# Products of 64 rows in the two halves of TensorE's array, one transposition for two heads, and a second buffer for reloaded tiles

## The chip, the cores and the metric

One core of a Trainium2 chip runs the kernel once. The metric is the device time of that execution in microseconds; the time before is the median of three runs. Times inside a run come from one profiled execution. Engines are named as in the profile: PE is TensorE (PEld its weight loads), DVE is VectorE, ACT is ScalarE, POOL is GpSimd, SP is SyncE, whose queue issues most DMA transfers. Each engine works through its own list of instructions in a fixed order and waits where data or a buffer is not there yet.

## What is computed

One layer of an encoder: normalization and one wide projection, then three groups of heads side by side (attention to a memory, a convolution module, and two-way RWKV-7 time mixing), an output projection with residual, a mixture of 16 experts of which each takes 128 of the 1024 tokens, and a last normalization. The change touches the time mixing alone, and the residual that runs beside it. Per head the reference is a scan over time:

```python
def step(state, inp):
    r_t, w_t, k_t, v_t, kk_t, a_t = inp
    sa = jnp.einsum('bhij,bhj->bhi', state, -kk_t)
    state = (state * w_t[..., None, :]
             + sa[..., :, None] * (kk_t * a_t)[..., None, :]
             + v_t[..., :, None] * k_t[..., None, :])
    y_t = jnp.einsum('bhij,bhj->bhi', state, r_t)
    return state, y_t
```

It runs forward and backward over 1024 tokens for 6 heads of 64, and both results are added.

## The kernel before

**Chunks and units.** The scan is cut into chunks of C = 64 tokens. Two heads share the 128 partitions: head 0 of a pair in the lower 64 (`lo`), head 1 in the upper 64 (`hi`). A unit is one pair of heads and one half of the sequence for each direction d, with HC = 8 chunks per direction; 3 pairs and 2 halves make 6 units, u = 0 to 5. For each unit these steps run:

- `prep` makes AR (the columns that read the state, for both heads) and BK (b and k, the columns that write it, decayed to the chunk's start). BK before holds [partition, chunk, head, i, 64], and in head h's place only h's 64 partitions are filled; the other 64 were cleared once with POOL memsets (lines 668 and 669) and stay zero.
- `within` (line 845) makes the products within a chunk. A group is four chunks of one direction (q, d), four groups to a unit. For each head it takes a PSUM tile psA out of two buffers, fills it with four products of all 128 partitions (line 854; the zero half of BK picks the head), and DVE multiplies it by the mask of causality into AM (line 857).
- `prep2` transposes BK chunk by chunk and head by head on PE (line 870), ACT copies the result to BT (line 871), and v is brought into the layout of SV.
- `invert` inverts the triangular part of AM: ACT gathers blocks (line 895), DVE runs 31 steps of two instructions (lines 910 and 911), PE joins the blocks (lines 934 and 945).
- `chain` carries the state through 8 chunks, in three steps of PE each (psX, psSA, psS) with copies and additions on DVE and ACT in between (Xs, SV, S).

**The residual.** `residual` (line 1067) multiplies the first five blocks of the mixed heads, kept in DRAM as oT_d in a high and a low part, by the output projection: 4 column quarters of 8 token tiles, 32 tiles. Each tile loads two fo tiles (line 1083: fo0 from oT_d's high part, fo1 from the low), and the input part fx (line 1085); PE forms 15 products (lines 329 to 331), DVE adds fx (line 1089), and SP stores the sum (line 1090). FOB is the number of buffers of each fo tile.

**The order.** All steps are generators. A small planner, `run`, goes through the main steps (projections, then the chains of units 0 to 5, 24 steps each) and advances each filling step (within, invert, prep, prep2, residual) by its share of a window of main steps given by the R_ constants. The framework then sets each engine's final order from what was recorded. While chain u runs, PE's list thus mixes it with the products of unit u + 1, the preparation of u + 2 and the residual's tiles.

Of the kernel before, what the change touches and what calls it, by code (L numbers as in the profile page):

```python
# [12 lines left out]
F32 = mybir.dt.float32  # L13
# [3 lines left out]
ALU = mybir.AluOpType  # L17
# [3 lines left out]
P = 128  # L21
# [10 lines left out]
C = 64  # L32
NCH = S // C
HC = NCH // 2
# [12 lines left out]
    _n += _w  # L47
NPC = _n

FOB = 1  # L50
RW = 1
LB = 1
KB = 2
# [1 line left out]
FL = [0, 0, 0, 0, 0, 0, 0, 0]  # L55
# [45 lines left out]
def hybrid_block_kernel(ctx: ExitStack, tc: tile.TileContext, x, xT, memT, memn, w_in, w_mk, w_mv, pcols,  # L101
                        ups, gate_up, w_out, g_ffn, g_fin, w_router, w_eg, w_eu, w_ed, out, dbg=None):
    nc = tc.nc
    V, A, G, T = nc.vector, nc.scalar, nc.gpsimd, nc.tensor
# [12 lines left out]
    ident = const.tile([P, P], F32, name="ident")  # L117
# [16 lines left out]
    mask = const.tile([P, 2, C], F32, name="mask")  # L134
# [86 lines left out]
    def mm(tagp="mm", w=512, shape=None, name="mm", bufs=None):  # L221
        return psums[-1].tile(shape or [P, w], F32, name=name, tag=tagp, bufs=bufs or mmb[0].get(tagp))
# [270 lines left out]
    for n in range(2):  # L493
        ps = mm()
# [157 lines left out]
    Z = {}  # L652

    def early():

        ph1r.close()
        Z["se"] = pool("se", bufs=2, stack=ph2r, side="right")
        Z["pcs"] = [Z["se"].tile([P, 2, HC], F32, name=f"pcs{i}", bufs=1) for i in range(3)]
        Z["s1"] = pool("s1", bufs=2, stack=ph2e, side="right")
        Z["ew"] = pool("ew", bufs=1, stack=ph2e, side="right")  # L660
        ge = pool("ge", stack=ph2e, side="right")
        Z["AR"] = [ge.tile([P, 2, HC, 2, C], F32, name="AR0")]
        Z["AM"] = [ge.tile([P, 4, 2, 2, C], F32, name=f"AM{i}") for i in range(4)]
        Z["TT"] = [ge.tile([P, NCH, 2, 32], F32, name="TT0")]

        Z["BK"] = [ge.tile([P, HC, 2, 2, C], F32, name=f"BK{d}") for d in range(2)]
        for bk in Z["BK"]:
            G.memset(bk[hi, :, 0], 0.0)
            G.memset(bk[lo, :, 1], 0.0)
        Z["ep"] = ge.tile([P, HC, C + 1], F32, name="ep")  # L670
        G.memset(Z["ep"][:, :, 0:1], 1.0)
        Z["dinit"] = dinit = ge.tile([P, 16, 32], F32, name="dinit")
        G.iota(dinit, pattern=[[-2, 16], [1, 32]], base=0, channel_multiplier=0,
               allow_small_or_imprecise_dtypes=True)
        V.tensor_scalar(dinit, dinit, lpar1, None, op0=ALU.is_equal)

        rst = ge.tile([P, HC, C], F32, name="rst")
        V.memset(rst, 1.0)
        V.memset(rst[:, :, 0:1], 0.0)
        Z["rst"] = rst.rearrange("p a b -> p (a b)")  # L680
        yield
# [93 lines left out]
    def prep(p, k, g):  # L775
# [7 lines left out]
        for d in range(2):  # L783
# [36 lines left out]
            yield  # L820

            BK = g["BK", d] = Z["BK"][d]
            V.tensor_mul(BK[lo, :, 0, 0, :], kd[lo], cl[lo])
            (G, V)[FL[7]].tensor_mul(BK[hi, :, 1, 1, :], kd[hi], cl[hi])
            for r_, h, i in ((lo, 0, 1), (hi, 1, 0)):
                V.scalar_tensor_tensor(BK[r_, :, h, i, :], sg[r_], -0.5, cl[r_], op0=ALU.mult, op1=ALU.mult)  # L826
            yield
            both = chunks(pd["prod"][:, half(n)], d)
            if k == 0:
# [15 lines left out]
    def within(g):  # L845

        for q, d in ((0, 0), (0, 1), (1, 0), (1, 1)):
            AM = g["AM", d, q] = Z["AM"][g["u"] % 2 * 4 + q * 2 + d]
            for h in range(2):
                ps = mm("A", shape=[P, 4, 2, C], name="psA", bufs=2)  # L850
                r_ = slice(h * 64, h * 64 + 64)
                for c in range(4):
                    cc = q * 4 + c
                    T.matmul(ps[:, c].rearrange("p a b -> p (a b)"),  # L854
                             lhsT=g["BK", d][:, cc, h].rearrange("p a b -> p (a b)"),
                             rhs=g["AR"][:, d, cc].rearrange("p a b -> p (a b)"), start=True, stop=True)
                V.tensor_tensor(AM[:, :, h], ps, mask[:, None].to_broadcast([P, 4, 2, C]), op=ALU.mult)
                yield

    def prep2(p, k, g):  # L860
        BT = g["BT"] = Z["BT"][g["u"] % 2]
        SV = g["SV"] = Z["SV"][g["u"] % 2]
        for d in range(2):
            n = k if d == 0 else 1 - k

            for h in range(2):
                ps = mm(shape=[P, HC, C])
                r_ = slice(h * 64, h * 64 + 64)
                for cc in range(HC):
                    T.transpose(ps[:, cc, :], g["BK", d][r_, cc, h].rearrange("p a b -> p (a b)"), ident[r_, r_])  # L870
                A.copy(BT[:, d, :, h, :], ps)
                yield

            vt = load(f"v{p}", n, 1)
            if d == 1:
                vr = Z["sp"].tile([P, 512], F32, name="vr", bufs=1)
                G.tensor_scalar(vr, vt[:, ::-1], 1.0, None, op0=ALU.mult)
                vt = vr
            ps = mm(shape=[P, HC, C])
            for c in range(HC):  # L880
                for r_ in (lo, hi):
                    T.matmul(ps[r_, c, :], lhsT=vt[r_, c * C:(c + 1) * C], rhs=ident[r_, r_], start=True, stop=True)
            A.copy(SV[lo, d, :, 0, :], ps[lo])
            A.copy(SV[hi, d, :, 1, :], ps[hi])
            yield
# [762 lines left out]
```

## Time and profile before

| what | value |
|---|---|
| median of 3 runs | 1496.11 us (1487.31 to 1499.1) |
| profiled execution | 1507.9 us, span 1506.2 us |
| PE busy | 1350.8 us, 90% of the span |
| PE weight loads busy | 1063.8 us, 71% |
| DVE busy | 1180.6 us, 78% |
| ACT busy | 809.0 us, 54% |
| POOL busy | 266.2 us, 18% |

The profiled execution has its own time, a little above the median; a sum made from its rows is to be held against 1507.9 us. PE's clock is granted at one of two levels, 1.2 or 2.4 GHz, and the profile gives the share of full speed in each stretch: about 1.0 in the expert stage and 0.76 to 0.89 in most of the RWKV stage. A float32 product stands as two records on PE, a transposition as one, and a record's duration contains its way through the array, so records that overlap are counted by their starts and ends.

The program has three stages: the projections up to about 360 us, with convolution, attention and the first unit's preparation; the six units up to about 850 us; routing and experts until the end.

### The profile page before, as it was taken

What the parts mean: (1) busy time and instruction counts of PE and PEld (TensorE: products, weight loads), DVE (VectorE), ACT (ScalarE), POOL (GpSimd) and SP (SyncE); (2) the same over time, 40 slices, a digit from 0 to 9 for tenths busy, and PEclk for the clock granted to TensorE, in tenths of its full rate; (3) what the DMA queues carried; (4) which work ended last, traced back from release to release, by engine and by line L of the source; (5) the groups of instructions that cost most, each with busy time, mean ns of one, the idle gap of its engine ahead of it and who ended that gap; (6) DMA issues with size and microseconds to landing.
All of it is one profiled execution on the core that took longest, in us unless ns stands there. A gap on an engine that the chain in (4) does not pass through costs nothing.

```text
span 1506.2 us, 24148 instructions
## 1 busy us (share of the span) xinstructions
PE 1350.8 (90%) x9178; PEld 1063.8 (71%) x9178; DVE 1180.6 (78%) x2089; ACT 809.0 (54%) x1200; POOL 266.2 (18%) x238
## 2 busy tenths in 40 slices
PE   6888999997899888878999729999999999999995
PEld 4776657675777776667868628877777778877772
DVE  7899975699687869596833679988888888878875
ACT  4222574433535243433322418888787887767774
POOL 2233223432121212130221000000001101111000
PEclk9999999998889788887999859999999999999998
DMA  8222112412443433342473758999999999999975
GB/s 290 71 62 65 64 64 105 140 70 72 140 142 107 140 104 120 89 120 86 137 268 141 293 181 322 374 356 379 380 380 368 378 379 381 371 355 356 378 281 201
DMA packets 146100, 327.91 MB, mean 218 GB/s; under 512 B 9792, under 2 KB 64960, under 8 KB 145984
## 3 DMA queue, kind: packets, MB, share of 16 engines
q1 hardware_dynamic: 139360, 303.14, 54.9%
q0 software_dynamic: 6192, 22.55, 5.2%
q8 instruction: 72, 1.18, 0.3%
q10 hardware_dynamic: 432, 0.68, 0.1%
q14 instruction: 44, 0.36, 0.1%
HBM read 288.58 MB, written 37.75 MB: 217 GB/s over the span
## 4 chain that ended last, share of the span: by engine, by line
PE 62%; DVE 21%; ACT 5%; DMA 5%; issue 4%; POOL 1%; SPq 0%; POOLq 0%; ACTq 0%; DVEq 0%
PE mm L330 14%; PE mm L329 14%; PE mm L331 14%; PE mm L1455 3%; DVE cv L517 3%; DVE dtmp L910 2%; DVE Dt L911 2%; PE mm L1438 2%; DMA fo<-oT_d 2%; PE psA L854 1%; ACT Ld L895 1%; PE mm L745 1%; PE mm L1165 1%; PE psS L988 1%; DVE BK L826 1%
## 5 line engine op out<-in xcount | busy, mean ns | idle before, releaser
L1355 DVE SCALAR_TENSOR_TENSOR ewl<-eraw,pc,ewh 128x1024 fp32r<-128x1024 f32 x256 | 319.7, 1280 | 72.8 <-ACT ewh L1354 65.8
L1354 ACT ACTIVATE ewh<-eraw,pc 128x1024 fp32r<-128x1024 f32 x256 | 288.6, 1150 | 47.6 <-PE mm L331 46.2
L330 PE MATMUL mm<-ewl,xh 128*128 128x512 f32 x512 | 202.0, 394 | 1.7 <-DVE ewl L1355 1.6
L329 PE MATMUL mm<-ewh,xh 128*128 128x512 f32 x512 | 200.3, 409 | 1.0 <-ACT ewh L1354 1.0
L331 PE MATMUL mm<-ewh,xl 128*128 128x512 f32 x512 | 200.1, 391 | 0.0
L329 PE MATMUL mm<-hh,wh 128*128 128x512 f32 x304 | 127.0, 418 | 10.2 <-ACT hh L310 10.2
L330 PE MATMUL mm<-hl,wh 128*128 128x512 f32 x304 | 126.9, 417 | 0.2
L331 PE MATMUL mm<-hh,wl 128*128 128x512 f32 x304 | 126.2, 415 | 0.8 <-POOL wl L325 0.8
L330 PEld LDWEIGHTS mm<-ewl,xh 128*128 128x128 f32 x512 | 96.6, 189 | 26.1 <-DVE ewl L1355 5.2
L329 PEld LDWEIGHTS mm<-ewh,xh 128*128 128x128 f32 x512 | 96.3, 188 | 24.3 <-issue 4.1
L1351 DVE TENSOR_TENSOR ewl<-eraw,ewh 128x1024 fp32r<-128x1024 f32 x90 | 106.1, 1220 | 7.0 <-ACT ewh L1350 5.5
L331 PEld LDWEIGHTS mm<-ewh,xl 128*128 128x128 f32 x512 | 96.3, 188 | 20.0 <-DVE xl L1443 0.2
L1350 ACT ACTIVATE ewh<-eraw 128x1024 fp32r<-128x1024 f32 x90 | 92.5, 1058 | 10.8 <-PE mm L331 9.3
L1483 POOL DMA_INDIRECT x_d<-ye,idx x15 | 25.8, 1722 | 345.8 <-ACT ye L1482 345.8
L325 POOL TENSOR_TENSOR wl<-wraw,wh 128x512 fp32r<-128x512 f32 x38 | 57.9, 1527 | 129.2 <-ACT wh L324 111.4
L329 PEld LDWEIGHTS mm<-hh,wh 128*128 128x128 f32 x304 | 59.7, 196 | 26.5 <-ACT hh L310 10.7
L330 PEld LDWEIGHTS mm<-hl,wh 128*128 128x128 f32 x304 | 59.8, 197 | 18.0 <-DVE hl L311 2.9
L910 DVE TENSOR_TENSOR dtmp<-Lt,Dt 128x126 f32<-128x126 f32 (+22 forms) x186 | 70.5, 379 | 2.7
L517 DVE SCALAR_TENSOR_TENSOR cv<-u,cw,cv 128x512 f32<-128x512 f32 (+1 forms) x87 | 72.2, 860 | 0.1
L331 PEld LDWEIGHTS mm<-hh,wl 128*128 128x128 f32 x304 | 59.8, 197 | 16.3 <-POOL wl L325 3.2
L330 PE MATMUL mm<-ewl,fh 128*128 128x512 f32 x180 | 70.8, 393 | 0.1
L331 PE MATMUL mm<-ewh,fl 128*128 128x512 f32 x180 | 70.1, 389 | 0.0
(421 smaller groups left out, 2969.4 us busy)
## 6 DMA issues: line engine op xcount, KB each, us to landing
eraw<-in_w_eg_dram SPq DMA_DIRECT2D x64, 1024.0 KB, 10.2
eraw<-in_w_eu_dram SPq DMA_DIRECT2D x64, 1024.0 KB, 10.7
eraw<-in_w_ed_dram SPq DMA_DIRECT2D x64, 1024.0 KB, 8.1
fo<-oT_d SPq DMA_DIRECT2D x64, 320.0 KB, 3.9
wraw<-in_w_in_dram SPq DMA_DIRECT2D x38, 256.0 KB, 2.8
ld_k<-d_k SPq DMA_DIRECT2D x18, 256.0 KB, 3.3
ld_v<-d_v SPq DMA_DIRECT2D x18, 256.0 KB, 3.4
xk<-in_xT_dram SPq DMA_DIRECT2D x16, 256.0 KB, 4.9
```

Of the source, the lines that this page charges most:

```text
L325: G.tensor_sub(wl, raw, wh.bitcast(F32))
L329: T.matmul(ps, lhsT=lh, rhs=rh, start=first, stop=False)
L330: T.matmul(ps, lhsT=lh, rhs=rl, start=False, stop=False)
L331: T.matmul(ps, lhsT=ll, rhs=rh, start=False, stop=last)
L517: V.scalar_tensor_tensor(o[:, 0:ln], z, w, o[:, 0:ln], op0=ALU.mult, op1=ALU.add)
L910: IE.tensor_tensor(tmp[:, sg, ts], lcol, drow, op=ALU.mult)
L911: IE.tensor_tensor(Dt[:, sg, ts], Dt[:, sg, ts], tmp[:, sg, ts], op=ALU.add)
L1350: A.activation(h, raw[a], AF.Copy)
L1351: V.tensor_sub(l, raw[a], h.bitcast(F32))
L1354: A.activation(h, raw[a], AF.Copy, scale=gain)
L1355: V.scalar_tensor_tensor(l, raw[a], gain, h.bitcast(F32), op0=ALU.mult, op1=ALU.subtract)
L1455: T.matmul(acc[n], lhsT=xw[:, k - KT + NWHOLE], rhs=h[:, sl], start=k == 0, stop=k == KT - 1)
```

## The change

BK loses its head dimension: head 0's b and k stand in the lower 64 partitions of [partition, chunk, i, 64], head 1's in the upper 64, nothing is zero, and the memsets go. In `within`, both heads' PSUM tiles are taken at once, and the eight products of a group run over 64 partitions each, alternating between the lower and the upper half; the two masks follow. In `prep2`, one transposition of 128 by 128 turns both heads of a chunk, four chunks to a PSUM tile, and two copies per direction remain. The freed memory holds a second buffer for each fo tile (FOB = 2).

```diff
--- before.py
+++ after.py
@@ -47,7 +47,7 @@
     _n += _w
 NPC = _n
 
-FOB = 1
+FOB = 2
 RW = 1
 LB = 1
 KB = 2
@@ -662,11 +662,7 @@
         Z["AR"] = [ge.tile([P, 2, HC, 2, C], F32, name="AR0")]
         Z["AM"] = [ge.tile([P, 4, 2, 2, C], F32, name=f"AM{i}") for i in range(4)]
         Z["TT"] = [ge.tile([P, NCH, 2, 32], F32, name="TT0")]
-
-        Z["BK"] = [ge.tile([P, HC, 2, 2, C], F32, name=f"BK{d}") for d in range(2)]
-        for bk in Z["BK"]:
-            G.memset(bk[hi, :, 0], 0.0)
-            G.memset(bk[lo, :, 1], 0.0)
+        Z["BK"] = [ge.tile([P, HC, 2, C], F32, name=f"BK{d}") for d in range(2)]
         Z["ep"] = ge.tile([P, HC, C + 1], F32, name="ep")
         G.memset(Z["ep"][:, :, 0:1], 1.0)
         Z["dinit"] = dinit = ge.tile([P, 16, 32], F32, name="dinit")
@@ -820,10 +816,10 @@
             yield
 
             BK = g["BK", d] = Z["BK"][d]
-            V.tensor_mul(BK[lo, :, 0, 0, :], kd[lo], cl[lo])
-            (G, V)[FL[7]].tensor_mul(BK[hi, :, 1, 1, :], kd[hi], cl[hi])
-            for r_, h, i in ((lo, 0, 1), (hi, 1, 0)):
-                V.scalar_tensor_tensor(BK[r_, :, h, i, :], sg[r_], -0.5, cl[r_], op0=ALU.mult, op1=ALU.mult)
+            V.tensor_mul(BK[lo, :, 0, :], kd[lo], cl[lo])
+            (G, V)[FL[7]].tensor_mul(BK[hi, :, 1, :], kd[hi], cl[hi])
+            for r_, i in ((lo, 1), (hi, 0)):
+                V.scalar_tensor_tensor(BK[r_, :, i, :], sg[r_], -0.5, cl[r_], op0=ALU.mult, op1=ALU.mult)
             yield
             both = chunks(pd["prod"][:, half(n)], d)
             if k == 0:
@@ -846,15 +842,15 @@
 
         for q, d in ((0, 0), (0, 1), (1, 0), (1, 1)):
             AM = g["AM", d, q] = Z["AM"][g["u"] % 2 * 4 + q * 2 + d]
+
+            ps = [mm("A", shape=[P, 4, 2, C], name="psA", bufs=2) for h in range(2)]
+            for c in range(4):
+                for h, r_ in ((0, lo), (1, hi)):
+                    T.matmul(ps[h][:, c].rearrange("p a b -> p (a b)"),
+                             lhsT=g["BK", d][r_, q * 4 + c].rearrange("p a b -> p (a b)"),
+                             rhs=g["AR"][r_, d, q * 4 + c].rearrange("p a b -> p (a b)"), start=True, stop=True)
             for h in range(2):
-                ps = mm("A", shape=[P, 4, 2, C], name="psA", bufs=2)
-                r_ = slice(h * 64, h * 64 + 64)
-                for c in range(4):
-                    cc = q * 4 + c
-                    T.matmul(ps[:, c].rearrange("p a b -> p (a b)"),
-                             lhsT=g["BK", d][:, cc, h].rearrange("p a b -> p (a b)"),
-                             rhs=g["AR"][:, d, cc].rearrange("p a b -> p (a b)"), start=True, stop=True)
-                V.tensor_tensor(AM[:, :, h], ps, mask[:, None].to_broadcast([P, 4, 2, C]), op=ALU.mult)
+                V.tensor_tensor(AM[:, :, h], ps[h], mask[:, None].to_broadcast([P, 4, 2, C]), op=ALU.mult)
                 yield
 
     def prep2(p, k, g):
@@ -863,12 +859,11 @@
         for d in range(2):
             n = k if d == 0 else 1 - k
 
-            for h in range(2):
-                ps = mm(shape=[P, HC, C])
-                r_ = slice(h * 64, h * 64 + 64)
-                for cc in range(HC):
-                    T.transpose(ps[:, cc, :], g["BK", d][r_, cc, h].rearrange("p a b -> p (a b)"), ident[r_, r_])
-                A.copy(BT[:, d, :, h, :], ps)
+            for q in range(2):
+                ps = mm(shape=[P, 4, P])
+                for c in range(4):
+                    T.transpose(ps[:, c, :], g["BK", d][:, q * 4 + c].rearrange("p a b -> p (a b)"), ident)
+                A.copy(BT[:, d, q * 4:q * 4 + 4].rearrange("p c h t -> p c (h t)"), ps)
                 yield
 
             vt = load(f"v{p}", n, 1)
```

The order of instructions moves as follows. First SP, in the residual, tiles 4 and 5 (fo_3732 and fo_3849 are the high parts of tiles 4 and 5, each with its low part under the next number; the stores are those of tiles 3 and 4). Before:

```order
L1083 DMA fo_3732<-oT_d_134 128x5x128
L1090 DMA xacc_d<-fx 128x256
L1083 DMA fo_3733<-oT_d_135 128x5x128
L729 DMA ld_k_3559<-d_k_146 128x512
L729 DMA ld_r_3561<-d_r_147 128x512
L1085 DMA fx<-in_x_dram 128x256
L729 DMA ld_v_3877<-d_v_145 128x512
L1083 DMA fo_3849<-oT_d_134 128x5x128
L1090 DMA xacc_d<-fx 128x256
L1083 DMA fo_3850<-oT_d_135 128x5x128
```

And now, at tiles 5 and 6 (fo_3814 is the low part of tile 5, fo_3911 and fo_3912 are tile 6; the stores are those of tiles 3 and 4):

```order
L1078 DMA fo_3813<-oT_d_134 128x5x128
L1078 DMA fo_3814<-oT_d_135 128x5x128
L1085 DMA xacc_d<-fx 128x256
L725 DMA ld_k_3539<-d_k_146 128x512
L725 DMA ld_r_3541<-d_r_147 128x512
L725 DMA ld_v_3841<-d_v_145 128x512
L1080 DMA fx<-in_x_dram 128x256
L1078 DMA fo_3911<-oT_d_134 128x5x128
L1078 DMA fo_3912<-oT_d_135 128x5x128
L1085 DMA xacc_d<-fx 128x256
```

The loads of a tile stood around the store of the tile before it; now they stand around the store of the tile before that one, one tile earlier.

Next PE, where the last two groups of unit 3's products lie, within the chain's last steps of one unit and the first of the next (BK_1940 and BK_1941 are the two directions, L1031 the start of the group normalization, L753 the sums of squares). Before:

```order
L854 MATMUL psA<-AR_1934,BK_1940 128x128 x2
L1031 MATMUL mm<-y,bd_79 128x512
L854 MATMUL psA<-AR_1934,BK_1940 128x128 x2
L854 MATMUL psA<-AR_1934,BK_1941 128x128 x4
L753 MATMUL mm<-bd_75,ksq 128x2 x4
L981 MATMUL psSA<-Xs,TT_1939 64x64 x4
L854 MATMUL psA<-AR_1934,BK_1941 128x128 x4
L753 MATMUL mm<-bd_75,gsq 128x2 x4
```

And now:

```order
L849 MATMUL psA<-AR_1934,BK_1940 128x128 x2
L1026 MATMUL mm<-y,bd_79 128x512
L849 MATMUL psA<-AR_1934,BK_1940 128x128 x6
L749 MATMUL mm<-bd_75,ksq 128x2 x4
L976 MATMUL psSA<-Xs,TT_1939 64x64 x4
L749 MATMUL mm<-bd_75,gsq 128x2 x4
L849 MATMUL psA<-AR_1934,BK_1941 128x128 x8
```

A group's products were cut into two tiles of four, with other work between; now the eight of a group, in alternating halves, stand together more often, and the next group follows after three other entries.

Last DVE in the new order, between the two masks of one group of unit 3 (AM_2999; dtmp and Dt are the inversion of another unit, S and Xs the chain):

```order
L853 TENSOR_TENSOR AM_2999<-psA,mask 128x4x128
L905 TENSOR_TENSOR dtmp<-Lt,Dt 128x12x8
L986 SCALAR_TENSOR_TENSOR S_4718<-psS,pcs_1923,sps 128x64
L906 TENSOR_TENSOR Dt<-Dt,dtmp 128x12x8
L986 SCALAR_TENSOR_TENSOR S_4718<-psS,pcs_1923,sps 128x64
L905 TENSOR_TENSOR dtmp<-Lt,Dt 128x13x7
L1009 TENSOR_TENSOR fb<-mm,ld_v_4861 128x512
L906 TENSOR_TENSOR Dt<-Dt,dtmp 128x13x7
L968 COPY Xs<-psX 128x128
L905 TENSOR_TENSOR dtmp<-Lt,Dt 128x13x6
L853 TENSOR_TENSOR AM_2999<-psA,mask 128x4x128
```

Nine entries stand between the masks of head 0 and head 1; before, nine stood there as well, and the next group's first product on PE needed the first of them alone.

## Rows read from the trace of the kernel before

**Rows 1.** Table of stretches: us, busy us of each engine (instructions), granted clock, DMA share, GB/s.

```profile
core 0: us, PE busy (x) PEld busy (x) DVE busy (x) ACT busy (x) POOL busy (x), PEclk, DMA share, GB/s
350.00:750.00 400.00, 344.33 (x4162) 282.31 (x4161) 311.48 (x812) 161.43 (x319) 80.00 (x83) 0.83 0.39 116
...
900.00:1506.00 606.00, 583.71 (x2592) 455.92 (x2590) 501.86 (x514) 458.30 (x507) 53.92 (x32) 0.99 0.94 351
```

**Rows 2.** Chain of waits, 350 to 750 us, shares of the chain by line.

```profile
by line: DVE dtmp L910 6.8%; DVE Dt L911 6.6%; DMA fo<-oT_d 6.4%; ACT Ld L895 5.3%; issue 5.1%; PE mm L331 4.5%; PE mm L329 4.5%; PE psA L854 4.0%; PE mm L330 3.7%; DVE BK L826 3.4%; PE psS L988 3.1%; PE mm L745 2.6%; DVE BK L823 2.2%; ACT
```

**Rows 3.** Who waited for whom, 350 to 750 us: us in total, times, longest.

```profile
PE mm L331 <- DMA fo<-oT_d: 6.3, 6, 2.0
PE mm L329 <- DMA fo<-oT_d: 6.1, 7, 1.7
...
PE psA L854 <- DVE AM L857: 1.0, 2, 0.6
DVE fx L1089 <- PE mm L331: 26.1, 17, 4.3
DVE Xs L973 <- PE psX L971: 8.2, 11, 2.3
```

**Rows 4.** Instructions on the fo tiles: ns min/median/max, first and last start in us.

```profile
L331 PE MATMUL mm<-fwh,fo x160: 274/283/681, 395.1 to 749.0; 128*128 128x256 f32 x160
...
DMA to landing us min/median/max: 3.2/3.9/6.2
```

**Rows 5.** Columns as in rows 1: stretch with a wait for fo, stretch behind.

```profile
530.30:533.70 3.40, 1.43 (x26) 1.23 (x23) 3.22 (x6) 2.24 (x2) 0.00 (x0) 1.00 0.38 117
533.70:537.10 3.40, 3.40 (x18) 3.28 (x16) 2.83 (x6) 0.00 (x0) 0.40 (x1) 0.50 0.09 26
...
632.70:636.10 3.40, 1.93 (x12) 0.90 (x12) 2.87 (x10) 0.95 (x2) 0.00 (x0) 1.00 0.44 129
636.10:639.50 3.40, 3.14 (x14) 2.92 (x14) 0.95 (x2) 1.26 (x2) 0.00 (x0) 0.50 0.00 1
```

**Rows 6.** PE in order of time (start, us, operation), and that stretch as in rows 1.

```profile
317.43 1.95 PE L854 MATMUL psA<-AR,BK 128*128 128x128 f32 x16
...
317.40:319.20 1.80, 1.80 (x18) 1.77 (x16) 0.92 (x4) 1.01 (x3) 0.00 (x0) 1.00 0.61 248
```

**Rows 7.** PE in order of time: attention scores of two heads together, and of one.

```profile
162.77 0.70 PE L608 MATMUL mm<-khT,oT 64*128 64x256 f32 x4
...
179.97 0.70 PE L608 MATMUL mm<-khT,oT 64*128 64x256 f32 x2
```

**Rows 8.** Instructions on psA: ns min/median/max, first and last start.

```profile
L854 PEld LDWEIGHTS psA<-AR,BK x128: 186/192/338, 301.1 to 548.0; 128*128 128x128 f32 x128
...
L857 DVE TENSOR_TENSOR AM<-psA,mask x48: 633/688/692, 304.6 to 699.8; 128x512 f32<-128x512 f32 x48
```

**Rows 9.** Groups by form, 350 to 800 us: busy us, mean ns, idle before.

```profile
L870 PE MATMUL mm<-ident,BK 64*128 64x64 f32 x192 | 21.4, 260 | 1.2 <-ACT sg L793 1.2
```

**Rows 10.** PE in order of time, changes of the array's part (rows*columns).

```profile
437.41 0.33 PE L969 MATMUL psX<-SVa,AM 64*64 64x64 f32 x4
437.67 0.34 PE L870 MATMUL mm<-ident,BK 64*128 64x64 f32 x2
...
438.49 0.58 PE L870 MATMUL mm<-ident,BK 64*128 64x64 f32 x6
439.25 0.45 PE L981 MATMUL psSA<-Xs,TT 64*64 64x64 f32 x8 [0.18 <-DVE Xs L973]
439.63 0.39 PE L329 MATMUL mm<-fwh,fo 128*128 128x256 f32 x1
439.86 0.28 PE L330 MATMUL mm<-fwl,fo 128*128 128x256 f32 x1
```

**Rows 11.** Instructions of one of the two lines that clear BK, ns, starts.

```profile
L668 POOL MEMSET BK<- x2: 944/945/946, 272.7 to 274.7; 64x1024 f32 x2
```

## Prediction

> **What bounds the kernel now.** I read the table of stretches first [rows 1]. The expert stage (900 to 1506 us) keeps TensorE (PE) busy 583.7 of 606 us at a granted clock of 0.99, and nothing of the change is in it. The change lives in the RWKV stage, 300 to 750 us. From 350 to 750 us PE is busy 344.3 us of 400 and VectorE (DVE) 311.5, at a mean granted clock of 0.83: neither engine is full, and both work through a fixed order, so each waits for the other and for loads. Then the chain of waits of that stretch [rows 2]: the two lines of the inversion on DVE (L910, L911) hold 13.4% of it, the loads of the fo tiles 6.4% (25.6 us), the psA products 4.0% (16 us). Then who waited for whom [rows 3]: PE stood 6.3 + 6.1 = 12.4 us in 13 waits for fo, and DVE stood 26.1 us at the addition of the residual tile (fx, L1089), which sits behind the same products; nothing else made DVE wait longer. Last the residual's tiles with their loads [rows 4], and busy time and granted clock around four of those waits [rows 5].
>
> **The change part by part.** The sum is made against the profiled execution, 1507.9 us. It is 0.8% above the median of the runs (1496.11), so at the end the result is scaled by 1496.11/1507.9 = 0.992.
>
> *A, the psA products.* There are 6 units with 4 groups (q, d) of 8 products, 192 in all, 128 columns each. A product leaves two records. Sixteen records back to back took 1.95 us at full clock [rows 6], so a product takes 1.95/8 = 0.244 us of PE. Now each uses 64 rows of the array, and lower and upper half alternate. What two halves do together is in the trace already: the attention scores are such products, with 64 rows and 128 array columns. One alone (two records) took 0.70 us; the two heads' products released at the same moment (four records) took 0.70 us too [rows 7]. So two neighbours of different halves go side by side. In the new order on PE the 192 products stand in 57 stretches with nothing in between; a stretch of n takes n/2 slots, rounded up. There are 16 of one product, 11 of two, 8 of three, 7 of four, 3 of five, 4 of six, 1 of seven and 7 of eight: 16 + 11 + 16 + 14 + 9 + 12 + 4 + 28 = 110 slots in place of 192. The 82 saved are worth 0.244/0.83 = 0.29 us each at the stage's mean clock: 24 us of PE's time. The Trainium skill, TensorEngine Tiling (Array Packing), section Theoretical Speedup, gives up to 2x where the contraction is 64 or less. By that 96 slots would be saved, 28 us; the order, with its stretches of one and three, gives 24 us, and I stay with the order.
>
> *B, the transpositions.* 192 of 64 columns become 96 of 128 columns, so the same number of columns passes. They are busy for 21.4 us in the stage [rows 9]. ScalarE (ACT) copies the same number of full tiles, each after 4 transpositions and no longer after 8. I take 0, with 2 us to either side.
>
> *C, changes of the array's division.* psA leaves the full array (128x128) that the fo products around it use, while the transpositions join it. Over PE's whole order there are 414 places where the part of the array changes before, and 455 after: 41 more. From a 64x64 product to a fo product the ends lie 440.02 - 439.70 = 0.32 us apart, where two fo products in a row lie 440.14 - 440.02 = 0.12 apart: 0.20 us for the change [rows 10]. Into a 64x128 product it is less: two records end 438.01 - 437.74 = 0.27 us after the product ahead, where six in a row take 0.58, under 0.1 each: 0.08 or a little more [rows 10]. I take 0.15, between the two: 41 x 0.15 = 6 us lost. Below: 0, where PE waits at that place anyway. Above: 41 x 0.2 = 8. The Trainium skill, same page, section Key Properties, speaks against the change here: any switch of the tiling mode drains TensorE, whatever the kinds. By that all 41 cost the 0.20 us measured for the one kind, 8 us; by the rows it is 6.
>
> *D, two PSUM tiles at once.* Before, PE filled psA of head 1 while DVE masked head 0. Now a group needs both of psA's two buffers, and the next group's upper product waits for the second mask; behind it in PE's fixed order stand the chain's products, and DVE waits for these. A mask takes 0.69 us [rows 8], so both are ready some 1.4 us after the group's last product. Of the 18 places where one group of a unit follows another, 11 have at most five entries of PE's order between; such a piece covers about half of that, an estimate from records of 0.12 to 0.4 us. 11 x 0.7 = 8 us lost. Below: 0. Above: 18 x 1.4 = 25 us. Before, this wait was worth 1.0 us [rows 3].
>
> *E, two places for fo.* The loads land 3.2 to 6.2 us after their issue [rows 4]. Before, SyncE (SP) could issue tile i + 1 only when PE was through with tile i. Now the loads of i + 1 stand in SP's order ahead of the store of i - 1 or right around it, so they have a whole tile's time, about 11 us (32 tiles in 355 us [rows 4]). I take all 12.4 us of PE's wait as gone. The clock comes on top. In four stretches with such a wait PE was busy 1.4 to 1.9 of 3.4 us at clock 1.0, and the next 3.4 us were granted 0.50, the 1.2 GHz level (two of the four pairs stand in [rows 5]). At that level half of a stretch is lost: 4 x 1.7 = 7 us. Together 19 us. Below: 12.4. Above: the chain's 25.6 us.
>
> *F, the rest.* Four POOL memsets of 0.94 us fall away, from 272.7 us on [rows 11]; they were done long before the tile's first product at 301 us [rows 8], worth 0. The BK writes on DVE and POOL keep their sizes.
>
> **Sum.** Counted as PE's time: -24 + 6 + 8 - 19 = -29 us. That is too much if PE, once faster, runs into DVE's order. Counted along the chain: psA's 16 us shrink by 82/192, so -7, fo gives -26, and C and D cost 14 again: -19 us. Both counts are partly right, and I take the middle, -24 us: 1507.9 - 24 = 1484, times 0.992 is 1472 us, 1.6% faster.
>
> **The rivals.**
> - *No difference: PE's gain turns into waits for DVE.* For it speaks that the inversion holds 13.4% of the chain, more than fo and psA together (10.4%), and that DVE is busy 78% of the stage. Against it speaks that DVE's longest wait is itself the one behind fo. If A's 24 us are used up by C (6), D (8) and 10 us of new waits for DVE, and of E the 12.4 us alone are regained, it is 1507.9 - 12 = 1496, or 1484 on the median's scale.
> - *Slower: the pair of PSUM buffers.* In DVE's new order up to 10 other instructions stand between a group's two masks. While DVE is there PE's order stands at the next group's upper product. To turn the sum to 15 us slower the 18 places must lose 39 us more than D counts, 47 us in all, 2.6 us each: two masks (1.4) and some 1.2 us of other DVE work. At 2.8 us each (50 us) it is 1507.9 - 24 + 42 = 1526, or 1514 on the median's scale. For it speaks that each such wait could also pull the clock down, as in [rows 5]; against it, that the next group's products already stand later in PE's order where the masks stand apart, and that psA's wait for a mask was only 1.0 us [rows 3].
> - *The halves do not run side by side in a stream*, because their weight loads (0.19 us a record [rows 8]) queue up. Then A is 0, C and D stay, E holds: -19 + 14 = -5 us, 1503, or 1491. Against it: in [rows 7] both loads were in the pair's 0.70 us.
>
> **How the numbers follow.** A measurement of this kernel can tell about 1% (15 us) from no change. The forecast and its neighbours down to -53 us (A 28, E 25.6, C and D nothing) hold 62%; the two cases without a difference, DVE's waits and the halves one after the other, 28%; the slower one 10%. The range reaches from 1450 (some -47 us, short of that lower end) to 1497, which takes in both cases without a difference and leaves out the slower one. Faster 0.62, same 0.28, slower 0.10; the likeliest case's own range is 1450 to 1481.
>
> **What would show it.** A: psA's sixteen records of a group of eight within about 1.1 us at full clock, and PE's busy time from 300 to 750 us lower by about 20 us. C: idle times of PE ended by issue ahead of psA, some tenths of a us each. D: PE waits at psA for the AM masks, 5 to 10 us in all. E: no PE wait for fo left, DVE's wait at fx under 10 us, a mean clock from 350 to 750 us above 0.83. The expert stage should begin some 24 us earlier and keep its length. The forecast is wrong if PE's waits for Xs, S and SV on DVE grow by what fo gave up, or if psA waits for AM by tens of us.

## The result, and the profile after

The changed kernel takes 1517.24 us (median of 4 runs, 1512.58 to 1520.34) where the kernel before takes 1492.17 (4 runs beside it): a ratio of 1.013, 95% interval 1.0085 to 1.0175. On a second chip it was 1.0103 (1.0063 to 1.0142). It is slower by a little over 1%, where 1.6% faster was forecast. Where one execution of a kernel was over 1.5% longer than the fastest of the same kernel, as one of the four of e8 below, it is left out of the ratios, medians and means. The profiled run of after took 1520.34 us with a span of 1518.6. The profiled run of before took 1507.9 us, longer than any of the four executions in its median (1487 to 1499), so tables of the two traces side by side show less than the whole difference.

Line numbers in after are four or five lower than in before (psA L854 is now L849, the masks L857 are L853, fx L1089 is L1084). The table of stretches of after, answering to [rows 1]; the expert stage begins 12 us later:

```profile
350.00:750.00 400.00, 344.02 (x3995) 272.90 (x3993) 304.24 (x790) 159.03 (x317) 75.87 (x82) 0.79 0.39 116
912.00:1518.00 606.00, 584.08 (x2594) 456.29 (x2592) 502.46 (x514) 458.51 (x507) 54.41 (x32) 0.99 0.94 351
```

The expert stage is as it was (584 us busy, 0.99). In the RWKV stage PE is exactly as busy as before, 344 us, but gets less done: 3995 records for 4162, of which up to 96 are transpositions that the change does away with. DVE does less too (790 for 812), and the granted clock is 0.79 in place of 0.83. That is one execution each; over the timed runs the clock of the whole run is 0.907 for after and 0.924 to 0.926 for before. Who waited for whom in that stretch, answering to [rows 3]:

```profile
DVE fx L1084 <- PE mm L331: 22.8, 12, 8.7
DVE AM L853 <- PE psA L849: 11.7, 12, 2.9
DVE Xs L968 <- PE psX L966: 10.3, 10, 3.0
PE psSA L976 <- DVE Xs L968: 9.1, 9, 2.2
...
PE psA L849 <- DVE AM L853: 1.3, 3, 0.6
...
PE mm L331 <- DMA fo<-oT_d: 0.8, 1, 0.8
```

PE's waits for fo are gone (12.4 to 0.8 us) and psA hardly waits for a mask (1.0 to 1.3 us). But DVE's wait at fx only fell from 26.1 to 22.8 us, and summed over all lines of this view PE's waits are what they were: 54.7 us before, 55.4 after. Its waits for DVE rose from 26.3 to 35.0. The chain of the stretch, answering to [rows 2], names fo no more and psA with 6.0% in place of 4.0:

```profile
by line: DVE Dt L906 7.5%; DVE dtmp L905 7.3%; PE psA L849 6.0%; issue 5.0%; ACT Ld L890 4.4%; PE mm L329 4.4%; PE mm L331 3.6%; PE mm L330 3.6%; PE psS L983 3.3%; DVE BK L822 3.0%; PE mm L749 2.7%; DVE BK L819 2.4%; PE mm L940 2.3%; PE psS
```

PE in order of time shows the best and a poor group of psA, sixteen records each (two a product), answering to [rows 6]:

```profile
299.42 1.16 PE L849 MATMUL psA<-AR,BK 64*128 64x128 f32 x16 [1.39 <-DVE BK L819]
...
388.23 3.31 PE L849 MATMUL psA<-ARa,BK 64*128 64x128 f32 x16 [1.40 <-DVE BK L819]
```

In the first the halves alternate and go side by side: 1.16 us where [rows 6] has 1.95. In the second, at half clock, four products of the lower half run one after the other and then four of the upper, with little overlap: 3.31 us, where side by side eight times a record's 0.21 us would be 1.7.

The half-clock periods are where the loss can be seen. Before, the longest between the first and the last step of the chain was 13.7 us. After, two last 30.7 us each (23.9 us in e11, the same kernel again), in which PE is busy 92 and 96% of the time and is still granted 0.50, the 1.2 GHz level:

```profile
593.40:624.10 30.70, 28.28 (x263) 24.66 (x263) 20.22 (x61) 7.12 (x12) 3.69 (x5) 0.50 0.25 76
689.00:719.70 30.70, 29.40 (x285) 23.25 (x286) 14.06 (x43) 11.51 (x27) 2.07 (x3) 0.50 0.14 40
```

From the chain's first Xs to its last the stage takes 417.0 us where it took 406.3. Of that 158 us are at half clock, before 116 (e11: 414.8 and 149). Counted with half-clock time as half it fell, from 348 to 338 us, but this doesn't show work taken from PE: counted so, of the runs below e2, which has hardly any pairs, comes to 339 as well, and e3, with the products of before, to 364.

### The profile page after: what moved, and what is told of

It is laid out like the page before. It is cut to its first block, busy times and chain, and to the rows that moved or that the text cites. A ratio compares the mean times of both kernels' runs of the same rounds, so it can differ in the third digit from the quotient of the medians.

```text
span 1518.6 us, 23980 instructions
## 1 busy us (share of the span) xinstructions
PE 1362.2 (90%) x9082; PEld 1063.0 (70%) x9082; DVE 1180.7 (78%) x2089; ACT 808.8 (53%) x1200; POOL 258.5 (17%) x234
## 3 DMA queue, kind: packets, MB, share of 16 engines
q8 instruction: 71, 1.16, 0.3%
## 4 chain that ended last, share of the span: by engine, by line
PE 63%; DVE 22%; ACT 5%; DMA 4%; issue 4%; POOL 1%; SPq 0%; POOLq 0%; ACTq 0%; DVEq 0%
PE mm L329 14%; PE mm L330 14%; PE mm L331 14%; PE mm L1450 3%; DVE cv L517 3%; DVE dtmp L905 3%; DVE Dt L906 3%; PE psA L849 2%; PE mm L1433 2%; ACT Ld L890 1%; PE psS L983 1%; PE mm L1160 1%; PE mm L749 1%; DVE BK L822 1%; PE mm L608 1%
```

## The experiments

Theories: (R) products on half the rows bring the granted clock down; (P) the two PSUM tiles taken at once make PE wait; (O) PE's order leaves too few neighbours of different halves; (V) VectorE's order bounds the stage, so freed waits only move. The last columns are means over the timed runs: the clock of the whole run, and twice (1 - clock) times the span, the time at half clock.

| kernel | median us | ratio to before (95%) | clock, before's | us at half clock, before's |
|---|---|---|---|---|
| e1 after, one place for fo | 1526.0 | 1.0146 (1.009-1.020) | 0.901, 0.924 | 303, 228 |
| e2 after, one PSUM tile at a time | 1528.6 | 1.0150 (1.010-1.020) | 0.901, 0.924 | 301, 228 |
| e3 before, both tiles at once | 1502.4 | 1.0010 (0.997-1.005) | 0.927, 0.924 | 219, 228 |
| e4 after, products tied | 1509.0 | 1.0061 (1.003-1.010) | 0.912, 0.924 | 266, 228 |
| e5 after, all 128 rows | 1497.3 | 1.0015 (0.999-1.004) | 0.932, 0.926 | 204, 220 |
| e6 as e5, one place for fo | 1502.8 | 1.0038 (0.999-1.009) | 0.925, 0.926 | 226, 220 |
| e7 before, row halves alone | 1525.7 | 1.0221 (1.018-1.026) | 0.899, 0.926 | 308, 220 |
| e8 e4 with full-row products added | 1518.2 | 1.0158 (1.008-1.023) | 0.918, 0.926 | 248, 220 |
| e10 tied, own PSUM place a half | 1509.8 | 1.0095 (1.006-1.013) | 0.914, 0.926 | 260, 221 |
| e11 after again | 1512.6 | 1.0103 (1.006-1.014) | 0.912, 0.926 | 265, 221 |
| e14 e10, each product twice | 1530.2 | 1.0199 (1.015-1.025) | 0.915, 0.922 | 259, 234 |

**The pair of PSUM tiles (P).** e3 edits the kernel before, e2 undoes the pair in the changed one.

```diff
 (e3)
-for h in range(2):
-    ps = mm("A", ...)
-    for c in range(4):
+ps = [mm("A", ...) for h in range(2)]
+for c in range(4):
+    for h in range(2):
         T.matmul(ps[h][:, c], lhsT=BK[:, q * 4 + c, h], rhs=AR[:, d, q * 4 + c])
```

e3: 

> The kernel before with one edit: both PSUM tiles of a group are taken at once and the two heads' products alternate, still on all 128 rows with their zero blocks. This is the cost of the two tiles by itself. The prediction's term was 8 us (bounds 0 and 25): 1500 us. If the pair of tiles is what made the changed kernel slow, 1505 to 1520 us with psA's waits for AM masks up by 5 us or more. If it costs nothing, within 5 us of before, and the row halves or the transpositions are to blame.

e2 is the changed kernel with the loop over h outside again, on 64 rows: 

> The changed kernel with one PSUM tile at a time again: the lower half's four products and their mask, then the upper half's, each still on 64 rows; full transpositions and two places for fo are kept. Pairs of halves go away nearly altogether, so PE loses what pairing still gives. If taking both PSUM tiles at once is what costs (waits for the second mask, idle PE, a lower clock), this run is 12 to 25 us faster than the changed kernel, 1492 to 1505 us, psA's waits for AM and BK shrink and the granted clock of 350 to 750 us rises from 0.79 to above 0.83. If the cost lies in using half the rows (changes of the array's division, less of the array at work and so a lower clock), it stays at 1515 to 1530 with a clock of 0.79 or less.

e3 is the same as before (1.001), e2 no faster than after. The pair of tiles costs nothing that can be measured (at most 0.5%, e3), and P falls. e2 also says that the loss does not come from the alternation: on half rows without pairs it is as large.

**The rows, alone and undone (R).** e7 is e3 with one more edit, the rows:

```diff
-lhsT=BK[:, q * 4 + c, h], rhs=AR[:, d, q * 4 + c]
+lhsT=BK[r_, q * 4 + c, h], rhs=AR[r_, d, q * 4 + c]      (r_: lower or upper 64 rows)
```

> The kernel before with the row halves alone: both PSUM tiles at once (which alone gave a ratio of 1.001), products on 64 rows alternating, old transpositions, one place for fo, zero blocks left in place and unread. If the row halves are the cause, this run is 10 to 25 us slower than before (1510 to 1525 where before has 1500), with a mean clock over the run near 0.90 where before has 0.923. If the transpositions or the compact tile are, it is within 5 us of before or faster.

e5 goes the other way, from the changed kernel (`[r_, ...]` to `[:, ...]` in both operands): 

> The changed kernel with its psA products on all 128 rows again, from the dense BK and AR, so each gives the sum over both heads: the output is not the reference's (the mask is 0.1 in place of 1 so that values stay bounded); every other step, the two places for fo and the full transpositions are the change's. It costs the products of before, 192 of 0.24 us, with no pairs. If half the rows are what pulls the granted clock down, the clock of 350 to 750 us rises from 0.79 to 0.83 or more and the run takes 1485 to 1502 us although PE has more work. If PE's own time, the transpositions or the compact tile were the cause, it stays at 1510 to 1530.

The stretch 350 to 750 us of e3, e5 and e7, columns as in [rows 1]:

```profile
350.00:750.00 400.00, 340.80 (x4393) 278.98 (x4391) 313.86 (x821) 166.34 (x330) 85.32 (x87) 0.88 0.41 121
```
```profile
350.00:750.00 400.00, 339.40 (x4380) 272.42 (x4378) 311.69 (x818) 167.23 (x334) 83.78 (x90) 0.88 0.42 130
```
```profile
350.00:750.00 400.00, 349.24 (x3972) 280.44 (x3970) 296.52 (x764) 155.64 (x312) 79.33 (x80) 0.76 0.37 112
```

Between e3 and e7 only the rows differ: 1.001 against 1.022, clock 0.88 against 0.76, and PE is busier (349 us for 341) while it does less. PE's waits did not grow (49.8 us in e7, 57.9 in e3). With all rows back, e5 takes before's time. So the row halves alone make the kernel slower, and the rest of the change is worth nothing that can be measured. In e3 half of the weight rows are zeros, in e5 none are, and the clock is 0.88 in both (0.927 and 0.932 over the timed runs): the zeros made no difference to it that can be seen.

**Two places for fo (V).** `FOB = 1` in place of 2, in the changed kernel (e1) and in e5 (e6).

e1: 

> The changed kernel with one place for each fo tile again, all else of the change kept; the order on PE shifts a little with it (143 row-half slots for the 192 psA products in place of 145). If the second place is worth what the prediction gave it (12.4 us of PE's waits and the clock behind them), this run is 12 to 19 us slower than the changed kernel, near 1530 to 1536 us, and PE's waits for fo are back at about 12 us. If DVE's order bounds the stage, so that the waits only moved (DVE's wait at fx fell merely from 26.1 to 23.4 us), it is within 5 us of the changed kernel's 1517, and the loss against before lies wholly in the products and transpositions.

e6: 

> As the run on all 128 rows (sum over both heads, mask 0.1, output not the reference's), with one place for each fo tile: the second place by itself, where the clock is not pulled down by half rows. By the prediction's step on fo it is 12 to 19 us slower than with two places. By what the changed kernel showed (1517 with two, 1526 with one, on different chips) it is 0 to 8 us slower. Against the kernel before with both tiles at once (ratio 1.001 to before) it shows the full transposition alone: by the prediction the same within 2 us.

e6 against e5 is 1.0038 to 1.0015, e1 against after 1.0146 to 1.013 and, in e11, 1.0103: 2 to 6 us, within the intervals. Waits of 350 to 750 us, e6 first, then e5:

```profile
DVE fx L1084 <- PE mm L331: 21.7, 14, 6.0
PE mm L329 <- DMA fo<-oT_d: 7.6, 8, 1.7
...
PE mm L331 <- DMA fo<-oT_d: 2.9, 3, 2.4
```
```profile
DVE fx L1084 <- PE mm L331: 13.9, 11, 5.6
...
PE psA L849 <- DVE BK L822: 6.4, 4, 2.5
...
PE mm L331 <- DMA fo<-oT_d: 1.4, 2, 1.2
```

The second place takes 9 us of PE's waits for fo (10.5 to 1.4), and PE's waits for DVE grow by as much (29.0 to 37.8 over all lines). V holds for this part. What time the second place brings comes with 22 us less at half clock (226 to 204).

**PE's order (O).** Counted by which half stands next to which, the 192 products of the changed kernel take about 140 slots (139 if any two neighbours of different halves make a pair; the expectations say 145). Among the stretches are 11 single lower ones, and groups such as three lower, three upper, lower, upper. e4 ties each product behind the one before it, without a wait:

```diff
+last = None
 for c in range(4):
     for h, r_ in ((0, lo), (1, hi)):
-        T.matmul(...)
+        with issue_after(last):
+            last = T.matmul(...)
```

> The changed kernel with its eight products of a group tied in the order lower, upper, lower, upper on PE. In the changed kernel's order the halves often stand four lower, then four upper; counted by half, its 192 products take 145 slots, and tied 116. If the missed pairs are what the prediction's first term lost, this run saves 29 slots of 0.29 us, 8 us: about 1509 us, and the time psA takes on PE falls by that. If PE's own time is not what bounds the stage, or the tie makes PE wait longer for the second mask, it stays at 1517 or goes up, to 1517 to 1530.

e10 also gives each half its own PSUM place and starts with the upper half: 

> The changed kernel with its products tied more closely: the lower half's tile and the upper half's each have a PSUM place of their own, and a group starts with the upper half, whose place comes free last, so that little gets between: 107 slots for the 192 products, where the changed kernel has 145 and the tied one (1.0061 of before) 116. In the series on fixed data a half running alone kept the clock at 0.50 for all its 109.6 us and pairs ran at 1.00 from 5.1 us on. If lone halves are the cause, this run has a higher clock than the tied one (0.912 where before had 0.923) and is 3 to 8 us faster, 0.998 to 1.005 of before. If changes of the array's division or the chain's waits bound it, it stays at 1.006 or above.

e11 is its companion: 

> The changed kernel itself on the same chip as the tied version and before: 1.013 of before, mean clock near 0.907.

e4 came out as expected: 1509 us, 1.0061 of before, 0.4 and 0.7% below the two ratios of after, whose intervals overlap its own. e10 reached the tightest pairs: inside its stretches of psA without a break at full clock, a record ends 0.056 us after the one before (mean of 241), in after 0.072, before 0.112. Yet it is not faster than e4. Nor is it clearly faster than the changed kernel on the same chip (e11): 1509.8 us to 1512.6, and 260 us at half clock to 265. In its stage:

```profile
350.00:750.00 400.00, 334.92 (x4115) 263.04 (x4115) 309.44 (x812) 160.69 (x320) 80.43 (x84) 0.80 0.38 116
```

PE is busy 335 us where it was 344, the products do go two at a time, and PE's waits grew from 54.7 to 64.0 us, those for DVE from 26.3 to 48.4. So O is worth something between nothing (e10 against e11) and 10 us (e4), and even with nearly every pair in place (107 slots) the kernel is about 1% slower than before. The idea that lone halves by themselves cause the loss falls with e10.

**The clock by itself (R).** e9 runs products of psA's form on fixed data: `for c in range(512): half_(c)` with the halves in turn, then 256 with `lower(c)` only, and others.

> Not the kernel's work at all: the output is zeros, and PE runs eight series of products of psA's form on fixed data, each but the second after some 20 us of rest: (1) 256 on 128 rows, (2) at once behind them 512 on 64 rows, lower and upper half in turn, (3) the same 512 after a rest, (4) 256 on the lower 64 rows alone, (5) 2048 of the chain's form (64 rows, 64 columns), (6) 12 times 96 of the chain's form and 8 on 128 rows, (7) the same with 8 on 64 rows in turn, (8) and (9) as 6 and 7 with a wait on DVE behind each eight. If products on half the rows pull the granted clock down, series 4, 5, 7 and 9 show more time at 0.50 than 1, 6 and 8, and the pairs of 2 and 3 tell whether two halves at once count as a whole. If they don't, all series come to 1.00 within some us and stay there. A pair should take 0.11 us a record at full clock, as the products on 128 rows do for one.

Its first series (all rows, and pairs right behind), the pairs after a rest, and the lower half alone:

```profile
6.00:122.00 116.00, 116.00 (x1526) 115.88 (x1526) 0.00 (x0) 0.00 (x0) 1.00 0.08 30
143.00:202.00 59.00, 59.00 (x1022) 59.00 (x1020) 0.00 (x0) 0.00 (x0) 0.96 0.01 2
222.00:331.00 109.00, 108.91 (x510) 108.91 (x511) 0.04 (x1) 0.00 (x0) 0.50 0.00 1
```

One half without its partner, begun after a rest, kept PE busy for 109 us and was granted 0.50 to the end. Pairs, begun after a rest too, came to 1.00 after 5.1 us and stayed there. With a wait behind each eight (series 8 and 9) the clock fell once with all rows and nine times with pairs, but PE stood 1.55 us in the one and 1.77 in the other. So two more runs with equal waits.

e12: 

> Fixed data again, output zeros, none of the kernel's work. After 256 products on 128 rows come five series, each after a rest of some 20 us: 16 times (96 products of the chain's form, then a group, then a wait on DVE). The groups: (1) 8 products on 128 rows, (2) 8 on 64 rows, lower and upper in turn, (3) 16 of these, so as long on PE as the first, (4) 8 on 64 rows, four lower and then four upper, (5) nothing. Before, series 2's kind had nine falls to 0.50 and series 1's kind one. If half rows as such keep the clock down, 2, 3 and 4 all fall often. If it is the time for which the array works on all its rows, 3 stays up like 1 (0 to 2 falls), 2 and 5 fall often, and 4 falls at least as often as 2 though its group takes as long as the first.

The last series of e9, with the pairs, and the last of e12, which has no group between the chain's products and the wait:

```profile
848.00:964.00 116.00, 96.52 (x2460) 93.60 (x2460) 17.00 (x33) 0.00 (x0) 0.86 0.01 3
667.00:784.00 117.00, 91.22 (x3010) 89.17 (x3006) 23.20 (x45) 0.00 (x0) 1.00 0.01 3
```

With a group PE stood 0.5 to 0.7 us a round in e12 and the clock never fell, so the groups can't be told apart. Without one PE stood 1.72 us a round, and the clock did not fall either in 15 rounds, where e9's pairs with 1.77 us had nine falls. That speaks against the reading that less work on all rows before a wait is enough to lose the clock. e13 has longer waits:

```diff
+for n in (3, 4, 5):                                   # operations of DVE in the wait
+    series(lambda: [full(c) for c in range(8)], n)    # 8 on 128 rows
+    series(lambda: [half_(c) for c in range(8)], n)   # 8 on 64 rows, in turn
+    series(lambda: [half_(c) for c in range(16)], n)  # 16 on 64 rows, in turn
+    series(apart, n)                                  # 4 lower, then 4 upper
```

> Fixed data, output zeros. Twelve series of 12 times (96 products of the chain's form, a group, a wait on DVE), with three lengths of wait (3, 4 and 5 operations of DVE, so that PE stands about 1.5, 1.9 and 2.3 us), and four groups each: 8 products on 128 rows; 8 on 64 rows in turn; 16 on 64 rows in turn (as long as the first); 8 on 64 rows, four lower then four upper. With PE standing 0.5 to 0.7 us no group let the clock fall, with 1.55 to 1.77 us the 128 rows gave 0.98 and the pairs 0.86. If half rows as such pull the clock down, both series of pairs fall more than the 128 rows at each wait. If the length of the work on all rows decides, 16 in turn equal the 128 rows, and 8 in turn and 8 apart fall more.

The twelve series in this order, four to each wait (PE stands 1.44, 1.90 and 2.37 us); the third number from the right is the clock:

```profile
84.00:195.00 111.00, 95.14 (x2492) 92.23 (x2489) 14.09 (x33) 0.00 (x0) 0.98 0.01 3
216.00:316.00 100.00, 84.03 (x2494) 80.94 (x2490) 14.09 (x33) 0.00 (x0) 0.98 0.01 3
336.00:448.00 112.00, 96.03 (x2688) 93.11 (x2688) 14.10 (x33) 0.00 (x0) 0.97 0.01 3
469.00:582.00 113.00, 97.14 (x2483) 94.23 (x2480) 14.09 (x33) 0.00 (x0) 0.91 0.01 3
603.00:725.00 122.00, 101.06 (x2487) 98.16 (x2484) 18.79 (x44) 0.00 (x0) 0.92 0.01 3
747.00:867.00 120.00, 98.96 (x2472) 96.05 (x2472) 18.79 (x44) 0.00 (x0) 0.84 0.01 3
889.00:1008.00 119.00, 97.95 (x2666) 95.04 (x2664) 18.79 (x44) 0.00 (x0) 0.95 0.01 3
1030.00:1152.00 122.00, 101.07 (x2489) 98.15 (x2488) 18.79 (x44) 0.00 (x0) 0.88 0.01 3
1173.00:1296.00 123.00, 96.99 (x2496) 94.06 (x2492) 23.48 (x55) 0.00 (x0) 0.96 0.01 3
1318.00:1439.00 121.00, 94.89 (x2476) 91.97 (x2476) 23.48 (x55) 0.00 (x0) 0.87 0.01 3
1461.00:1583.00 122.00, 95.88 (x2676) 92.96 (x2674) 23.49 (x55) 0.00 (x0) 0.97 0.01 3
1605.00:1745.00 140.00, 113.99 (x2486) 111.08 (x2483) 23.48 (x55) 0.00 (x0) 0.78 0.01 2
```

At the two longer waits 8 in turn fare worse than 8 on all rows (0.84 and 0.87 against 0.92 and 0.96), and 16 in turn, which last as long as these (1.99 us), fare as well (0.95 and 0.97). At the shortest wait the three are alike. Four and four apart, which last 1.64 us where 8 in turn last 1.09, fare badly at every wait (0.91, 0.88, 0.78), though at the middle one 8 in turn fare worse still. So in e13 a pair holds the clock as a full product does for the time that it runs, and halves apart do not. These are single executions of about a dozen rounds each, and e12's series without a group doesn't fit. That the shorter time of the pairs loses the clock is thus not shown.

**The work put back.** e8 adds four useless products on all rows ahead of each group of e4, e14 doubles each product of e10 (`for c in (0, 1, 2, 0, 1, 2, 3, 3)`).

e8: 

> The changed kernel with the eight products of a group tied in the order lower, upper (which alone gave 1509 us, clock 0.912), and four useless products on all 128 rows put ahead of each group into the lower half's tile, overwritten by the real ones: 96 products, about 23 us of PE's time at full clock more. If the clock is what the row halves lose, PE's full-row work brings part of it back: clock of the run above 0.912, and the time no worse than 1509 in spite of the 23 us. If PE's time is what bounds the stage it is 1520 to 1532.

e14: 

> The version with a PSUM place for each half (1.0095 of before, clock 0.914 where before had 0.926), with every psA product issued twice: 384 products in about 206 slots, so that the array works in psA as long as before the change; some 24 us of PE's time more at full clock. If the time for which the array works is what holds the clock, the clock comes back to 0.92 or more and the time stays within 5 us of the version with single products. If half rows are what counts against it, the clock stays at 0.914 or falls, and the time rises by 10 to 24 us.

Both bring at most part of the clock back. e14's distance to before shrinks from e10's 0.012 to 0.007, e8's from e4's 0.012 to 0.008, and the stretch 350 to 750 us of e14 goes from 0.80 to 0.83. Both cost more than that gives: the time rose by about 15 us over e4 and e10. By their expectations the times are those of the second alternative (e8, by its ratio, within 1520 to 1532, e14 within 10 to 24 us more), and e14's clock is short of the 0.92 that the first asked for. What the added work gives back in clock is less than its price in PE's time.

## Why the prediction was wrong, step by step

- **A, the psA products: mis-sized, and its price was missing.** The count of slots let any two neighbours go side by side. It had to ask which half each uses: about 140 slots and not 110, some 52 saved and not 82, at 0.244 us 13 us of PE at full clock. Tying regained 10 us at most (e4), by e10 against e11 about 3. What failed altogether is the step "worth 0.29 us each at the stage's mean clock", which takes the clock as given. On half rows the mean fell, from 0.83 to 0.79 in the two traces and from 0.88 to 0.76 between e3 and e7. The 42 us more at half clock between the first Xs and the last cost PE up to 21 us (an estimate: half of them), nearly the 24 us that A was to bring. The Trainium skill, TensorEngine Tiling (Array Packing), section Theoretical Speedup, states up to 2x for a contraction of 64 or less. e10's 0.056 us a record against 0.112 agrees, and e10 is slower than before nevertheless.
- **B, the transpositions: right as far as can be seen.** e6 (with them) is 1.0038 of before and e3 (without) 1.0010; the intervals overlap.
- **C, changes of the array's division: right, at the upper end.** PE of after in order of time, at full clock:

```profile
409.88 0.28 PE L330 MATMUL mm<-fwl,fo 128*128 128x256 f32 x1
410.00 0.28 PE L331 MATMUL mm<-fwh,fo 128*128 128x256 f32 x1
410.20 0.49 PE L849 MATMUL psA<-ARa,BK 64*128 64x128 f32 x2
```

  In the trace's records the first psA record ends 0.303 us after the fo product, and the second 0.113 after the first: 0.19 us for the change, 8 us for 41 places. At all 29 such places at full clock in after, 16 behind the full array and 13 behind 64x64 products, it is 0.302 to 0.304, so the 0.08 us that the prediction read for the second kind was too small. The Trainium skill, same page, section Key Properties, states that a change of the tiling mode drains TensorE. The 29 places agree, in that both kinds of change cost the same.
- **D, both PSUM tiles at once: 8 us were counted, nothing can be measured** (e3, 1.001 with 0.997 to 1.005, and psA's 1.3 us of waits for masks). The slower rival named the right side and the wrong mechanism.
- **E, two places for fo: right about the waits, wrong about the time.** The waits went (12.4 to 0.8 us), and PE's waits for DVE took their place (26.3 to 35.0). E brought 2 to 6 us of the 19. That is the first rival's mechanism, which held for this part. The step that failed is adding PE's waits, and the clock behind them, in full, with DVE busy 78% of the stage.
- **The sum.** It took the middle of two counts that both left the clock alone. Of its signs psA's group in 1.1 us appeared (1.16, but rarely), and PE's waits for fo went. psA's waits for masks stayed at 1.3 us where 5 to 10 were named, DVE's wait at fx at 22.8 where under 10 was, and the expert stage came 12 us later and not 24 earlier. PE's busy time did not fall, and a clock above 0.83 turned into 0.79: the prediction's own test, and the one that failed plainly.

Over the kernels on half rows without added products the time rises by a quarter to somewhat over a third of the added half-clock time (e7: 33 us for 88; e1: 22 for 75; e2: 22 for 73; e4: 9 for 38; after again: 15 for 44; e10: 14 for 39). The kernel before shows the same relation by itself: its 53 executions beside these runs have 200 to 259 us at half clock, and a straight line through them (correlation 0.92) rises by 0.33 us of time for each us. By that line, drawn on to 308 us, all these kernels and after itself lie within 4 us, and e10 within 1 us. The kernels on all rows (e3, e5, e6) lie 3 to 5 us above it, e8 and e14, with work added, 12 and 18. So the loss, e10's last 1% included, goes with the time at half clock, and no extra loss by waits for DVE is needed to account for it. Which of the two comes first such a line cannot show.

That the row halves cause the loss is shown (e7 against e3, e5 against after). That a half alone, after a rest, is left at half clock is shown on fixed data. What in the row halves brings the clock down in the kernel stays open: shorter work before a wait, the few lone halves that e10 leaves, or the changes of the array's division. These changes rise with the halves, from 435 in e3 to 482 in e7 and from 412 in e5 to 455 in after. At 0.19 us that is 8 or 9 us of PE's time, against some 30 and 17 us lost, and no run has the halves without them. What the chain would do at an undisturbed clock stays open too. None of the versions beats the kernel before.

## What to carry to other kernels

The price of a product at the stage's mean clock holds only while that clock stays as it is. Here it fell with the rows that the products used, so try such a change alone first, and compare the granted clock along with the time. When counting products that share the array, go through the order half by half; neighbours alone say nothing, and products that should run in pairs have to be tied. And a wait removed from an engine that meets a second busy engine at every step can come back as a wait for that one, as 9 us did here.

## What the runs showed of the hardware

PE busy without a break with products on the lower 64 rows alone was granted 0.50 for 109 us after a rest (e9), while pairs of halves, and the chain's small products of 64 rows and 64 columns on alternate halves, were granted 1.00 after some 5 us. Two halves side by side do run at twice the rate (0.056 us a record in e10 for 0.112 before), their weight loads included, when they alternate. Four lower and then four upper took 1.64 us, where 8 in turn took 1.09 and 8 on all rows 1.98 (e13). A change into the 64x128 division costs 0.19 us at full clock (after, 29 places).
